# Turning attention probabilities from a rounded-kind view of the score tile, with explicit waits on their writers

## The chip, the cores and the metric

The kernel runs on one core of one Trainium2 chip. The metric is the device time of one execution in microseconds (us); the time before is the median of three runs. A core has a matrix engine (TensorE, PE in the profile, with its weight loads listed apart as PEld), a vector engine (VectorE, DVE), a scalar engine (ScalarE, ACT), a general engine (GpSimd, POOL) and a sequencer that only issues DMAs (SyncE, SP). Each works through its own queue in order; semaphores tie the queues together. SBUF is the memory that engines work in, PSUM the one that TensorE writes.

## The reference, cut to what matters

One layer of an encoder is applied to two groups of tokens, 1024 and 256, with shared weights: `x + W_out @ concat[SSD, windowed attention, memory attention]` of the normalized `x`. The two attentions are what the change touches:

```
# windowed grouped-query attention, 8 heads, 2 key/value heads, blocks of 128 queries
logits = where(|t-s| <= 128, q.k * d**-0.5 - slope*|t-s|, -inf)
m      = max(max(logits), sink)
probs  = exp(logits-m) / (sum(exp(logits-m)) + exp(sink-m))
o_att  = (probs @ v) * silu(z_att)
...
# memory cross-attention, 4 heads, 256 memory rows
pm     = softmax(mq.mk * d**-0.5)
o_mem  = (pm @ mv) * silu(z_mem)
```

Everything is float32. The kernel keeps that accuracy in the large products by splitting each operand into a rounded part (kind `fp32r`) and a rest, and adding three products of such parts.

## The kernel before

**Tiling and stages.** The 1280 tokens are ten tiles of 128 (`NT = 10`), in two groups of five. Most of the time goes into the projections: `block_tok`, `block_feat` and `block_pair` walk the 2048 input features in steps, load a tile of weights (`wraw`, a ring of four buffers), let ACT round it (`wh`, L206) and DVE take the rest (`wl`, L207), and issue three matmuls per product (L258 to L260, L293 to L295, L1268 to L1270) into PSUM tiles `acc`.

**What runs beside them.** Attention and the SSD scan are generators that wait in two queues (`lanes`) and are advanced a few steps at each step of a projection (`pump`, rates in `RATES`). The instructions that a step issues go to their engines' queues among those of the projection. The final order on each engine is set by a scheduler that works from priorities and its own cost estimates, so a change of an instruction's kind or of a dependency can also swap neighbours elsewhere.

**The windowed attention,** `attn(t)`, runs once per token tile, from 637 to 1304 us of the profile. After the queries are normalized (POOL computes `qr` at L123, L124 and L637, DVE applies it at L641) it makes four rounds `rr`. In `scores(rr)` POOL copies the sink into the last column of a score tile `lg` (L665), TensorE makes the scores `psc` (L671, L672), DVE adds the distances and writes `lg` (L673), ACT takes the exponential in place (L677) and DVE scales it in place by the reciprocal of the sum (L681). In `turn_(rr)` TensorE turns the probabilities, 128 columns at a time, into the PSUM tile `ppt` (L693), and ACT copies that to `pT` (L694). `values` multiplies by the values (L703). With two or three key blocks per tile there are 4 or 6 turns per round, 208 in all.

**The memory attention,** `mem_attn(t)`, does the same in two rounds `hp` per token tile: ACT writes the exponentials `mpr` (L781), DVE scales them (L786), and TensorE turns them into `pmt` (L794), 8 per tile and 80 in all.

A turn is a matmul whose weights are the piece of the probabilities and whose moving operand is the identity. The identity lies in a tile of kind `fp32r`, `identr`; `ident` is the same memory seen as float32. The turns of queries, keys, gates and SSD tiles (`pq` L653, `pk` L536, `pmq` L744, `pxs` L889, `pd` L1074, `pz` L1088) already use `identr` with an operand of kind `fp32r`; those of the probabilities and of the SSD result (`pr` L1038) use `ident` with a float32 operand.

Score tiles of both attentions come from one ring of two buffers with the tag `lg`, which a row of scales, `rbc`, also uses for a while. A tile's buffer is given to the next tile once every reader of the old one is done; the first instruction that writes into the buffer waits for that.

Of the kernel before, what the change touches and what calls it, by code (L numbers as in the profile page):

```python
# [10 lines left out]
F32 = mybir.dt.float32  # L11
F32R = mybir.dt.float32r
# [4 lines left out]
ALU = mybir.AluOpType  # L17
AX = mybir.AxisListType

P = 128  # L20
# [24 lines left out]
def hymba_encoder_kernel(  # L45
# [7 lines left out]
    V, A, G, T, S = nc.vector, nc.scalar, nc.gpsimd, nc.tensor, nc.sync  # L53
# [33 lines left out]
    identr = const([P, P], "identr", F32R)  # L87
    ident = identr.bitcast(F32)
# [87 lines left out]
    rbc = {}  # L176
# [440 lines left out]
        yield  # L617


    def attn(t):  # L620
        lo, hi = (0, NS) if t < NS else (NS, NT)
        k0, k1 = max(lo, t - 1), min(hi, t + 2)
        na = k1 - k0
        nk = na * P
        d0 = (k0 - (t - 1)) * P
        s0 = k0 if t < 4 else k0 - 3
        grp, ti = divmod(t, 5)
        tc_ = slice(ti * P, (ti + 1) * P)
        q = taken("attn", t)
        yield  # L630
        sq = w2("sq")
        A.activation(sq, q, AF.Square)
        ss = sm.tile([P, 8], F32, tag="s8", name="qss", bufs=4)
        V.reduce_sum(out=ss, in_=hv(sq), axis=AX.X)
        r = sm.tile([P, 8], F32, tag="s8", name="qr", bufs=4)
        rsqrt(r, ss, 1.0 / 64, 8)
        G.tensor_tensor(out=r, in0=r, in1=steep, op=ALU.mult)  # L637
        for _ in range(3):
            yield
        q3 = hv(q)  # L640
        V.tensor_mul(q3, q3, hb(r, 8, 64))  # L641
        yield
        qT = []
        for b in range(2):
            qh = mp.tile([P, 4, 2, 64], F32R, tag="wa", name="qh", bufs=WA)
            qb = q3[:, 4 * b:4 * b + 4, :]
            A.activation(qh[:, :, 0, :], qb, AF.Copy)
            V.tensor_sub(qh[:, :, 1, :], qb, qh[:, :, 0, :].bitcast(F32))
            yield
            ps = psum("pq")  # L650
            qf = qh.rearrange("p a b d -> p (a b d)")
            for a in range(4):
                T.transpose(ps[:, a * P:(a + 1) * P].bitcast(F32R), qf[:, a * P:(a + 1) * P], identr)  # L653
            o = mp.tile([P, 512], F32R, tag="qT", name="qT", bufs=2)
            A.activation(o, ps, AF.Copy)
            qT.append(o)
        z = w2("za")
        S.dma_start(hv(z, 4), zT_d[0][grp][:, :, tc_])
        yield
        ns8 = nsink.rearrange("p (v r) -> p r v", v=2)  # L660
        state_ = {}

        def scores(rr):
            lg = mp.tile([P, 2, 385], F32, tag="lg", name="lg", bufs=2)
            G.tensor_copy(lg[:, :, nk:nk + 1], ns8[:, rr, :].unsqueeze(2))  # L665
            nm = sm.tile([P, 2], F32, tag="m2", name="nm", bufs=10)
            for kv in range(2):
                h = 4 * kv + rr
                ps = psum("psc")
                st = qT[kv][:, rr * P:(rr + 1) * P]  # L670
                T.matmul(ps[:, :nk], st, kT[:, kv, s0 * P:s0 * P + nk], start=True, stop=False)  # L671
                T.matmul(ps[:, :nk], st, kL[:, kv, s0 * P:s0 * P + nk], start=False, stop=True)  # L672
                V.tensor_tensor_reduce(out=lg[:, kv, :nk], in0=pdist[:, d0:d0 + nk], in1=ps[:, :nk], scale=2.0 ** -(h + 1),  # L673
                                       scalar=nsink[:, h:h + 1], op0=ALU.add, op1=ALU.min, accum_out=nm[:, kv:kv + 1])
            den = sm.tile([P, 2], F32, tag="m2", name="den", bufs=10)
            for kv in range(2):
                A.activation(lg[:, kv, :nk + 1], lg[:, kv, :nk + 1], AF.Exp, scale=-1.0, bias=nm[:, kv:kv + 1],  # L677
                             accum_out=den[:, kv:kv + 1])
            V.reciprocal(out=den, in_=den)
            for kv in range(2):  # L680
                V.tensor_scalar(out=lg[:, kv, :nk], in0=lg[:, kv, :nk], scalar1=den[:, kv:kv + 1], scalar2=0.5,  # L681
                                op0=ALU.mult, op1=ALU.mult)
            state_[rr] = lg

        def turn_(rr):
            lg = state_.pop(rr)
            if rr % 2 == 0:
                state_["pT"] = mp.tile([P, 2, 2, 384], F32, tag="pT", name="pT", bufs=1)
            pT = state_["pT"]
            for kv in range(2):  # L690
                pt = psum("ppt")
                for a in range(na):
                    T.transpose(pt[:, a * P:(a + 1) * P], lg[:, kv, a * P:(a + 1) * P], ident)  # L693
                A.activation(pT[:, kv, rr % 2, :nk], pt[:, :nk], AF.Copy)  # L694

        oT = w2("oT")

        def values(half):
            pT = state_.pop("pT")
            po = psum("po")  # L700
            for a in range(na):
                for kv in range(2):
                    T.matmul(hv(po[kv * 64:kv * 64 + 64, :2 * P], 2), v_all[:, s0 + a, kv * 64:kv * 64 + 64],  # L703
                             pT[:, kv, :, a * P:(a + 1) * P], start=(a == 0), stop=(a == na - 1))
            c = slice(half * 2 * P, (half + 1) * 2 * P)
            V.tensor_mul(oT[:, c], po[:, :2 * P], z[:, c])

        scores(0)
        yield
        scores(1)  # L710
        yield
        yield
        turn_(0)
        yield
        scores(2)
        yield
        turn_(1)
        yield
        scores(3)
        yield  # L720
        values(0)
        yield
        turn_(2)
        yield
        turn_(3)
        yield
        fetch_next()
        yield
        values(1)
        yield  # L730
        S.dma_start(oT_d[0][grp][:, :, tc_], hv(oT, 4))


    def mem_attn(t):
# [29 lines left out]
        st_ = {}  # L764

        def scores(hp):
            ps = psum("pms")
            for j in range(2):
                h = 2 * hp + j
                c = slice(h * P, (h + 1) * P)  # L770
                o = ps[:, j * 256:(j + 1) * 256]
                T.matmul(o, qh[:, c], mkH[:, h, :], start=True, stop=False)
                T.matmul(o, qh[:, c], mkL[:, h, :], start=False, stop=False)
                T.matmul(o, ql[:, c], mkH[:, h, :], start=False, stop=True)
            m = sm.tile([P, 2], F32, tag="m2", name="mm", bufs=10)
            V.reduce_max(out=m, in_=hv(ps, 2), axis=AX.X)
            V.scalar_tensor_tensor(out=m, in0=m, scalar=-1.0, in1=r[:, 2 * hp:2 * hp + 2], op0=ALU.mult, op1=ALU.mult)
            pr = mp.tile([P, 512], F32, tag="lg", name="mpr", bufs=2)
            den = sm.tile([P, 2], F32, tag="m2", name="mden", bufs=10)
            for j in range(2):  # L780
                A.activation(pr[:, j * 256:(j + 1) * 256], ps[:, j * 256:(j + 1) * 256], AF.Exp,  # L781
                             scale=r[:, 2 * hp + j:2 * hp + j + 1], bias=m[:, j:j + 1], accum_out=den[:, j:j + 1])
            V.reciprocal(out=den, in_=den)
            for j in range(2):
                c = slice(j * 256, (j + 1) * 256)
                V.tensor_scalar(out=pr[:, c], in0=pr[:, c], scalar1=den[:, j:j + 1], scalar2=0.5,  # L786
                                op0=ALU.mult, op1=ALU.mult)
            st_[hp] = pr

        def turn_(hp):  # L790
            pr = st_[hp]
            pt = psum("pmt")
            for a in range(4):
                T.transpose(pt[:, a * P:(a + 1) * P], pr[:, a * P:(a + 1) * P], ident)  # L794
            if hp == 0:
                st_["pT"] = mp.tile([P, 2, 768], F32, tag="pT", name="mpT", bufs=1)
            pT = st_["pT"][:, hp, :512]
            A.activation(pT, pt, AF.Copy)
            st_[hp] = pT
# [659 lines left out]
    def x_rows(grp):  # L1459

        yield
        yield
        rbc[grp] = fin.tile([P, 640], F32, tag="rbc", name="rbc") if grp == 0 else \
            mp.tile([P, 640], F32, tag="lg", name="rbc", bufs=2)
        for o, n in ((0, 4), (4, 1)):
            ps = psum("prx")
            for i in range(n):
                t = 5 * grp + o + i
                T.matmul(ps[:, i * P:(i + 1) * P], rx[:, t:t + 1].broadcast_to([P, P]), ident, start=True, stop=True)
            V.tensor_copy(rbc[grp][:, o * P:(o + n) * P], ps[:, :n * P])  # L1470
        yield
# [289 lines left out]
```

## Time and profile before

| | |
|---|---|
| runs before, median of 3 (lowest, highest) | 1787.72 us (1787.32, 1790.27) |
| profiled execution, first to last instruction | 1784.2 us |
| median of the runs less that span | 3.5 us |
| TensorE busy | 1774.6 us, 99% of the span, 10838 matmuls |
| VectorE / ScalarE / GpSimd busy | 70% / 52% / 31% |
| granted TensorE clock, mean | 1.000 |

The profile holds one execution. Its times are counted from the first instruction; no time of that execution outside the span is recorded, so its own time is its span and whatever lies around it, for which the 3.5 us to the median of the runs is the only measure. A group row reads: line, engine, operation, what is written <- what is read, shape, count | busy time, mean duration in ns of one | idle time of the engine just before. Matmuls overlap in the array, so the duration of one is longer than the step from one to the next.

### The profile page before, as it was taken

What the parts mean: (1) busy time and instruction counts of PE and PEld (TensorE: products, weight loads), DVE (VectorE), ACT (ScalarE), POOL (GpSimd) and SP (SyncE); (2) the same over time, 40 slices, a digit from 0 to 9 for tenths busy, and PEclk for the clock granted to TensorE, in tenths of its full rate; (3) what the DMA queues carried; (4) which work ended last, traced back from release to release, by engine and by line L of the source; (5) the groups of instructions that cost most, each with busy time, mean ns of one, the idle gap of its engine ahead of it and who ended that gap; (6) DMA issues with size and microseconds to landing.
All of it is one profiled execution on the core that took longest, in us unless ns stands there. A gap on an engine that the chain in (4) does not pass through costs nothing.

```text
span 1784.2 us, 31407 instructions
## 1 busy us (share of the span) xinstructions
PE 1774.6 (99%) x10838; PEld 1606.3 (90%) x10838; DVE 1245.8 (70%) x2358; ACT 921.5 (52%) x2049; POOL 547.3 (31%) x900
## 2 busy tenths in 40 slices
PE   9999999999999999999999999999999999999999
PEld 7889999999998999999889977877988888899999
DVE  5596788888768887777665666557777644766665
ACT  5555455555434766756464565544447533533333
POOL 0105789999810100001001010000100000057775
PEclk9999999999999999999999999999999999999999
DMA  8654454445446644453635645557777764744442
GB/s 299 191 183 125 135 154 148 141 146 159 126 144 205 199 134 139 135 162 110 189 118 175 193 148 160 168 158 249 229 229 242 247 189 140 224 147 142 148 142 78
DMA packets 208207, 301.12 MB, mean 169 GB/s; under 512 B 19568, under 2 KB 86192, under 8 KB 208048
## 3 DMA queue, kind: packets, MB, share of 16 engines
q1 hardware_dynamic: 207904, 299.06, 54.5%
q8 instruction: 85, 1.39, 0.3%
q14 instruction: 74, 0.61, 0.1%
q10 hardware_dynamic: 144, 0.06, 0.0%
HBM read 236.36 MB, written 62.69 MB: 168 GB/s over the span
## 4 chain that ended last, share of the span: by engine, by line
PE 82%; issue 6%; DVE 4%; DMA 4%; POOL 2%; ACT 1%; SPq 0%; POOLq 0%; ACTq 0%; DVEq 0%
PE acc L258 9%; PE acc L260 8%; PE acc L259 8%; PE acc L1268 7%; PE acc L1270 7%; PE acc L1269 7%; PE acc L293 5%; PE acc L295 5%; PE acc L294 5%; PE accm L1268 3%; PE accm L1269 3%; PE accm L1270 3%; PE po L703 1%; PE ppt L693 1%; PE py L970 1%
## 5 line engine op out<-in xcount | busy, mean ns | idle before, releaser
L207 DVE TENSOR_TENSOR wl<-wraw,wh 128x512 fp32r<-128x512 f32 (+1 forms) x480 | 346.2, 723 | 244.0 <-ACT wh L206 238.5
L206 ACT ACTIVATE wh<-wraw 128x512 fp32r<-128x512 f32 (+1 forms) x480 | 292.2, 613 | 312.4 <-PE acc L260 147.8
L258 PE MATMUL acc<-wh,xH 128*128 128x512 f32 (+1 forms) x1088 | 418.9, 385 | 0.4 <-DVE v_all L337 0.4
L260 PE MATMUL acc<-wh,xL 128*128 128x512 f32 (+1 forms) x1088 | 410.1, 377 | 0.0
L259 PE MATMUL acc<-wl,xH 128*128 128x512 f32 (+1 forms) x1088 | 409.7, 377 | 0.0
L258 PEld LDWEIGHTS acc<-wh,xH 128*128 128x128 f32 x1088 | 204.5, 188 | 37.8 <-issue 3.4
L260 PEld LDWEIGHTS acc<-wh,xL 128*128 128x128 f32 x1088 | 204.4, 188 | 37.0 <-issue 0.2
L259 PEld LDWEIGHTS acc<-wl,xH 128*128 128x128 f32 x1088 | 204.7, 188 | 35.9 <-issue 1.6
L293 PE MATMUL acc<-xH,wh 128*128 128x320 f32 x640 | 202.8, 317 | 0.0
L294 PE MATMUL acc<-xL,wh 128*128 128x320 f32 x640 | 198.8, 311 | 0.0
L295 PE MATMUL acc<-xH,wl 128*128 128x320 f32 x640 | 198.0, 309 | 0.0
L206 ACT ACTIVATE sh<-ws 128x384 fp32r<-128x384 f32 x176 | 91.3, 523 | 204.8 <-POOL ws L1236 102.5
L207 DVE TENSOR_TENSOR sl<-ws,sh 128x384 fp32r<-128x384 f32 x176 | 123.8, 706 | 94.6 <-ACT sh L206 94.4
L1236 POOL TENSOR_TENSOR ws<-wraw 128x128 f32<-128x128 f32 x176 | 110.8, 630 | 205.8 <-DMA wraw<-in_w_in_pairs_dram 80.9
L665 POOL COPY lg<-nsink 128x2 f32<-128x2 f32 x40 | 13.6, 340 | 379.1 <-PE ppt L693 221.3
L1236 POOL TENSOR_TENSOR ws<-wraw,ws 128x128 f32<-128x128 f32 x176 | 118.7, 674 | 13.8
L293 PEld LDWEIGHTS acc<-xH,wh 128*128 128x128 f32 x640 | 120.2, 188 | 2.8 <-issue 2.2
L294 PEld LDWEIGHTS acc<-xL,wh 128*128 128x128 f32 x640 | 120.3, 188 | 1.7 <-issue 1.4
L295 PEld LDWEIGHTS acc<-xH,wl 128*128 128x128 f32 x640 | 120.2, 188 | 0.6 <-issue 0.5
L1236 POOL TENSOR_TENSOR wraw<-wraw 128x128 f32<-128x128 f32 x176 | 112.9, 642 | 13.7
L1236 POOL TENSOR_TENSOR ws<-ws,wraw 128x128 f32<-128x128 f32 x176 | 115.6, 657 | 0.0
L362 DVE SCALAR_TENSOR_TENSOR c<-u,vec,c 128x638 f32<-128x638 f32 (+1 forms) x96 | 90.0, 938 | 9.9 <-ACT c L357 9.5
(437 smaller groups left out, 3942.7 us busy)
## 6 DMA issues: line engine op xcount, KB each, us to landing
wraw<-in_w_in_laid_dram SPq DMA_DIRECT2D x176, 256.0 KB, 3.0
wraw<-in_w_in_pairs_dram SPq DMA_DIRECT2D x112, 256.0 KB, 2.7
wraw<-in_w_out_laid_dram SPq DMA_DIRECT2D x64, 256.0 KB, 3.5
wraw<-in_w_out_pairs_dram SPq DMA_DIRECT2D x64, 256.0 KB, 2.8
rf<-ac SPq DMA_DIRECT2D x40, 256.0 KB, 4.1
rb<-ac SPq DMA_DIRECT2D x40, 256.0 KB, 4.7
wraw<-in_w_mem_laid_dram SPq DMA_DIRECT2D x32, 256.0 KB, 4.4
xst<-in_x_sample_dram SPq DMA_DIRECT2D x20, 256.0 KB, 5.9
```

The lines of the kernel that those rows point to most:

```text
L206: a = A.activation(h, raw, AF.Copy)
L207: b = V.tensor_sub(l, raw, h.bitcast(F32))
L258: T.matmul(ps[t][:, :n], sh, h[:, :n], start=(k_ == 0), stop=False)
L259: T.matmul(ps[t][:, :n], sh, l[:, :n], start=False, stop=False)
L260: T.matmul(ps[t][:, :n], sl, h[:, :n], start=False, stop=(k_ == KT - 1))
L293: T.matmul(o, sh, cur["H", q][:, m, c], start=(k == 0), stop=False)
L294: T.matmul(o, sh, cur["L", q][:, m, c], start=False, stop=False)
L295: T.matmul(o, sl, cur["H", q][:, m, c], start=False, stop=(k == KT - 1))
L1236: G.tensor_tensor(out=o, in0=x, in1=y, op=op)
L1268: T.matmul(ps[p], h, xh, start=(k_ == 0), stop=False)
L1269: T.matmul(ps[p], h, xl, start=False, stop=False)
L1270: T.matmul(ps[p], l, xh, start=False, stop=(k_ == 7))
```

## The change

The probability tiles get a second name. After `scores` has written a tile, `turn_` asks the pool for a new tile of kind `fp32r` under the same tag, that is in the same memory, and turns from that with `identr` in place of `ident`. The tool that orders the instructions tracks tiles, not memory, so three things are added:

- each of the two buffers gets a tag of its own, `lg0` and `lg1`, with one buffer each, and the tiles take them in turn (`score_tile`); `rbc` of the second token group takes `lg0`;
- the new tile gets a writer of its own, a POOL memset of its last column (`as_words`), which lies outside what the turns read; it waits for all users of the old tile;
- each turn is told by hand to wait for the DVE instruction that scaled the piece it reads (`turn_words`).

The computed function is the same: turning does not change the words.

```diff
+    def score_tile(name, shape):
+        place[0] ^= 1
+        tag = f"lg{place[0]}"
+        return tag, mp.tile([P] + shape, F32, tag=tag, name=name, bufs=1)
+
+    def turn_words(out, words, wrote):
+        i = T.transpose(out.bitcast(F32R), words, identr)
+        for w in wrote:
+            tc.add_manual_dep(i.ins, w.ins.name, WRITTEN, reason="the words' writer")
+
+    def as_words(tag, name, shape):
+        w = mp.tile([P] + shape, F32R, tag=tag, name=name, bufs=1)
+        G.memset(w.bitcast(F32)[(slice(None),) + tuple(slice(n - 1, n) for n in shape)], 0.0)
+        return w
...
         def scores(rr):
-            lg = mp.tile([P, 2, 385], F32, tag="lg", name="lg", bufs=2)
+            tag, lg = score_tile("lg", [2, 385])
...
         def turn_(rr):
-            lg = state_.pop(rr)
+            tag, wrote = state_.pop(rr)
+            lg = as_words(tag, "lgw", [2, 385])
...
-                    T.transpose(pt[:, a * P:(a + 1) * P], lg[:, kv, a * P:(a + 1) * P], ident)
+                    turn_words(pt[:, a * P:(a + 1) * P], lg[:, kv, a * P:(a + 1) * P], wrote[kv:kv + 1])
...
-            pr = mp.tile([P, 512], F32, tag="lg", name="mpr", bufs=2)
+            tag, pr = score_tile("mpr", [512])
...
+            pr = as_words(tag, "mprw", [513])
...
-                T.transpose(pt[:, a * P:(a + 1) * P], pr[:, a * P:(a + 1) * P], ident)
+                turn_words(pt[:, a * P:(a + 1) * P], pr[:, a * P:(a + 1) * P], wrote[a // 2:a // 2 + 1])
...
-            mp.tile([P, 640], F32, tag="lg", name="rbc", bufs=2)
+            mp.tile([P, 640], F32, tag="lg0", name="rbc", bufs=1)
```

In the changed file the turns have line 632, the memset 639, the sink copy 687, the score matmuls 693 and 694, and the last step of `qr` 659.

**The turns on TensorE.** One round of the second token tile, `attn(1)`, with what each instruction waits for in brackets. Before:

```order
L295 MATMUL acc<-xH_7440,wl 128x320
L693 MATMUL ppt<-identr,lg 128x128 [waits DVE_49,Activation_49]
L693 MATMUL ppt<-identr,lg 128x128 x2
L693 MATMUL ppt<-identr,lg 128x128 [waits DVE_49]
L671 MATMUL psc<-kT,qT 128x384 [waits DVE_49]
L672 MATMUL psc<-kL,qT 128x384
```

The same place in the changed program:

```order
L295 MATMUL acc<-xH_7440,wl 128x320
L632 MATMUL ppt<-identr,lgw 128x128 [waits DVE_49,Activation_49]
L632 MATMUL ppt<-identr,lgw 128x128 x2
L632 MATMUL ppt<-identr,lgw 128x128 [waits DVE_49]
L693 MATMUL psc<-kT,qT 128x384 [waits DVE_49]
L694 MATMUL psc<-kL,qT 128x384
```

The place in the queue and the engines waited for are the same; no turn waits for POOL, since the memset writes a column that no turn reads.

**The memsets and sink copies on POOL.** The stretch from the queries' normalization of `attn(1)` to that of `attn(2)` (`qr` is the scale that DVE applies to the queries, `lg` a score tile, `lgw` its second name). Before:

```order
L637 TENSOR_TENSOR qr<-qr,steep 128x8
L665 COPY lg<-nsink 128x2 x4
L123 TENSOR_SCALAR qr<-qss 128x8
L124 TENSOR_TENSOR qr<-qr,mhalf 128x8
L637 TENSOR_TENSOR qr<-qr,steep 128x8
```

With the change:

```order
L659 TENSOR_TENSOR qr<-qr,steep 128x8
L687 COPY lg<-nsink 128x2
L639 MEMSET lgw 128x1 x2
L687 COPY lg<-nsink 128x2
L639 MEMSET lgw 128x1
L687 COPY lg<-nsink 128x2 x2
L639 MEMSET lgw 128x1
L687 COPY lg<-nsink 128x2
L123 TENSOR_SCALAR qr<-qss 128x8
L124 TENSOR_TENSOR qr<-qr,mhalf 128x8
L659 TENSOR_TENSOR qr<-qr,steep 128x8
```

Four memsets stand between the copies, and a fifth copy, that of the second round of `attn(2)`, has moved from behind that tile's `qr` chain to ahead of it. Elsewhere on POOL there is a memset for each of the 60 score tiles, and the neighbours keep their order but for three other exchanges of a copy with one instruction. On TensorE 34 matmuls stand some rows earlier or later; on DVE, ACT and SP some dozens of rows are exchanged with neighbours.

More of the change, by code (lines that the diff above doesn't have):

```diff
@@ L617, in dt_prep @@
         yield
+    place = [0]
+    def score_tile(name, shape):
+        place[0] ^= 1
+        tag = f"lg{place[0]}"
+        return tag, mp.tile([P] + shape, F32, tag=tag, name=name, bufs=1)
+    WRITTEN = mybir.DependencyInfo(mybir.DependencyClass.Sync, mybir.DependencyReason.DATA)
+    def turn_words(out, words, wrote):
[6 more added lines that the diff above has]
+        return w
     def attn(t):
@@ L679, in scores @@
             V.reciprocal(out=den, in_=den)
[L680 to L683, printed above, removed]
+            wrote = [V.tensor_scalar(out=lg[:, kv, :nk], in0=lg[:, kv, :nk], scalar1=den[:, kv:kv + 1], scalar2=0.5,
+                                     op0=ALU.mult, op1=ALU.mult) for kv in range(2)]
+            state_[rr] = tag, wrote
         def turn_(rr):
-            lg = state_.pop(rr)
+            tag, wrote = state_.pop(rr)
+            lg = as_words(tag, "lgw", [2, 385])
             if rr % 2 == 0:
@@ L783, in scores @@
             V.reciprocal(out=den, in_=den)
+            wrote = []
             for j in range(2):
                 c = slice(j * 256, (j + 1) * 256)
-                V.tensor_scalar(out=pr[:, c], in0=pr[:, c], scalar1=den[:, j:j + 1], scalar2=0.5,
-                                op0=ALU.mult, op1=ALU.mult)
-            st_[hp] = pr
+                wrote.append(V.tensor_scalar(out=pr[:, c], in0=pr[:, c], scalar1=den[:, j:j + 1], scalar2=0.5,
+                                             op0=ALU.mult, op1=ALU.mult))
+            st_[hp] = tag, wrote
         def turn_(hp):
-            pr = st_[hp]
+            tag, wrote = st_[hp]
+            pr = as_words(tag, "mprw", [513])
             pt = psum("pmt")
             for a in range(4):
-                T.transpose(pt[:, a * P:(a + 1) * P], pr[:, a * P:(a + 1) * P], ident)
+                turn_words(pt[:, a * P:(a + 1) * P], pr[:, a * P:(a + 1) * P], wrote[a // 2:a // 2 + 1])
             if hp == 0:
```

## Prediction

> **What bounds the kernel now.** I read the page first: busy times, the clock by slices, the chain that ended last.
>
> ```profile
> PE 1774.6 (99%) x10838; PEld 1606.3 (90%) x10838; DVE 1245.8 (70%) x2358; ACT 921.5 (52%) x2049; POOL 547.3 (31%) x900
> PEclk9999999999999999999999999999999999999999
> PE 82%; issue 6%; DVE 4%; DMA 4%; POOL 2%; ACT 1%; SPq 0%; POOLq 0%; ACTq 0%; DVEq 0%
> ```
>
> TensorE holds 82% of the chain, and its clock is full. Since its busy time is modelled, 99% alone proves little. The list of waits of TensorE is better evidence; it is short, and these are its longest entries:
>
> ```profile
> PE pmt L794 <- DVE mpr L786: 1.4, 2, 1.3
> PE warm L1544 <- DVE zero L1542: 1.3, 1, 1.3
> PE acc L1268 <- ACT qs L326: 0.8, 1, 0.8
> ```
>
> Idle time is 1784.2 - 1774.6 = 9.6 us in all, no DMA is among the releasers, and a turn of the probabilities waited 1.4 us in total. The stretch with all attention, one row of the table of windows (busy time of PE, PEld, DVE, ACT, POOL, then clock), says the same where the change lies:
>
> ```profile
> 637.00:1467.00 830.00, 826.88 (x5074) 717.38 (x5073) 561.62 (x1228) 467.77 (x1159) 66.39 (x120) 1.00 0.57 177
> ```
>
> TensorE idles 3.1 of 830 us; DVE has 268 us free, ACT 362, POOL 764. So what is taken off TensorE here should come off the end, and what is put on the others has room, unless a queue's order makes someone wait.
>
> **The turns.** The groups by shape give the counts, with two kinds of turn that already read `fp32r`:
>
> ```profile
> L693 PE MATMUL ppt<-identr,lg 128*128 128x128 f32 x208 | 31.2, 277 | 0.0
> L794 PE MATMUL pmt<-identr,mpr 128*128 128x128 f32 x80 | 11.4, 273 | 1.4 <-DVE mpr L786 1.4
> L1074 PE MATMUL pd<-identr,ydT 128*128 128x128 f32 x80 | 10.1, 249 | 0.5 <-DVE nm L673 0.5
> L653 PE MATMUL pq<-identr,qh 128*128 128x128 f32 x80 | 9.0, 246 | 0.0
> ```
>
> 288 turns change kind; 277 against 246 ns would be 31 ns each, or 8.9 us, but those are durations of overlapping matmuls. What counts is the time from the start of a group of turns until the matmuls behind it are back in step. I take it from the timeline, in four places where the projection L258 to L260 lies on both sides: from the start of the turns to the start of the second matmul after them. First float32 groups of 8 and 4, then `fp32r` groups of 8 and 4:
>
> ```profile
> 1438.94 1.03 PE L794 MATMUL pmt<-identr,mpr 128*128 128x128 f32 x8
> 1439.73 0.48 PE L258 MATMUL acc<-wh,xH 128*128 128x512 f32 x1
> 1440.05 0.39 PE L259 MATMUL acc<-wl,xH 128*128 128x512 f32 x1
> ...
> 1496.47 0.60 PE L1038 MATMUL pr<-identr,yd 128*128 128x128 f32 x4
> 1497.14 0.39 PE L259 MATMUL acc<-wl,xH 128*128 128x512 f32 x1
> ...
> 1065.84 0.79 PE L653 MATMUL pq<-identr,qh 128*128 128x128 f32 x8
> 1066.77 0.39 PE L259 MATMUL acc<-wl,xH 128*128 128x512 f32 x1
> ...
> 1486.56 0.46 PE L1074 MATMUL pd<-identr,ydT 128*128 128x128 f32 x4
> 1487.16 0.39 PE L259 MATMUL acc<-wl,xH 128*128 128x512 f32 x1
> ```
>
> Eight turns: 1440.05 - 1438.94 = 1.11 us against 1066.77 - 1065.84 = 0.93, so 0.18 less. Four: 0.67 against 0.60, so 0.07 less. An added float32 turn costs (1.11 - 0.67)/4 = 0.110 us, an added `fp32r` turn (0.93 - 0.60)/4 = 0.083. On the line through both, n turns in a row gain 0.0275 n - 0.04 us: 0.015 for 2, 0.04 for 3, 0.125 for 6. In the changed order of TensorE the windowed attention's turns stand in 22 groups of 6, 10 of 4, 6 of 3 and 9 of 2, the memory attention's in 5 of 8, 9 of 4 and 2 of 2; the sum is 22 x 0.125 + 19 x 0.07 + 6 x 0.04 + 11 x 0.015 + 5 x 0.18 = 2.75 + 1.33 + 0.24 + 0.17 + 0.90 = 5.4 us. All of it lies on the engine that bounds. The rate of 4 for all 288 turns gives 5.0 us, that of 8 gives 6.5; both round to the trace's hundredths.
>
> [...]
>
> **The waits on the turns.** A turn waited for DVE before and waits for DVE now, and takes no wait on POOL: nothing added on this path. The extra wait in the bound is that of each buffer's next writer, on the memset.
>
> **Sixty memsets on POOL,** not seen in this trace for this place. The nearest row is the sink copy, of similar size:
>
> ```profile
> L665 POOL COPY lg<-nsink x40: 181/188/942, 511.5 to 1288.4; 128x2 f32<-128x2 f32 x40
> ```
>
> At 0.19 us each they are 11.3 us of POOL's 764 free. Three parties can be held up. The next user of the buffer is DVE two score tiles later; the tightest case is here, between the scaling of one tile (L681) and the first write into the same buffer (the last row):
>
> ```profile
> 740.63 0.74 DVE L681 TENSOR_SCALAR lg<-lg,den 128x384 f32<-128x384 f32 x2
> 745.76 0.62 DVE L673 CUSTOM_DVE_ANT_0 lg<-pdist,psc,nsink 128x384 f32<-128x384 bf16 x1
> ```
>
> The memset can start at 741.4 and is due at 745.8: 4.4 us for 0.2. Next, the exponential needs the sink copy, which a memset may now precede; the tightest case:
>
> ```profile
> 785.49 0.51 POOL L665 COPY lg<-nsink 128x2 f32<-128x2 f32 x1 [24.98 <-PE ppt L693]
> 786.58 0.62 ACT L677 ACTIVATE lg<-lg,nm 128x385 f32<-128x385 f32 x1 [0.60 <-DVE nm L673]
> ```
>
> It is 0.58 us early, and before it POOL had been waiting 25 us, long enough for any memset. So I take zero for all sixty; the ends are zero and 11.3 us, the price if TensorE waited out each.
>
> [...]
>
> **The moved copy.** In `attn(2)` the second round's sink copy now precedes that tile's `qr` chain. It waits for the last turns of `attn(1)`, and behind it stand `qr`, then L641 on DVE, then whatever DVE does next:
>
> ```profile
> 702.74 0.82 PE L693 MATMUL ppt<-identr,lg 128*128 128x128 f32 x6
> ...
> 702.42 0.20 POOL L123 TENSOR_SCALAR qr<-qss 128x8 f32<-128x8 f32 x1 [2.03 <-DVE qss L634]
> 704.41 0.54 POOL L637 TENSOR_TENSOR qr<-qr,steep 128x8 f32<-128x8 f32 x1
> ...
> 704.99 0.69 DVE L641 TENSOR_TENSOR q<-q,qr 128x512 f32<-128x512 f32 x1
> 705.60 0.89 DVE L362 SCALAR_TENSOR_TENSOR c<-u,vec,c 128x646 f32<-128x646 f32 x1
> 707.64 0.69 DVE L207 TENSOR_TENSOR wl<-wraw,wh 128x512 fp32r<-128x512 f32 x1 [1.16 <-ACT wh L206]
> ```
>
> The turns end at 703.6, the copy at about 703.8, so L123 starts 1.4 us later than 702.42, and L641 and L362 with it. DVE then has 1.16 us of idle before the next weight split L207, which would come some 0.2 us late, with at least one split tile still ahead of TensorE. I take zero; the ends are zero and 1.4 us.
>
> **Other moves.** Neighbours are exchanged on SP, DVE, ACT and TensorE. TensorE waited for no DMA before, and each exchange is of one instruction (0.2 to 0.9 us in the rows above) whose sum of idle is 9.6 us over the whole run; I take 0 with ends of -2 and +3 us. Buffers that strictly alternate replace a ring of two: the tiles come and go in turn, so I take zero.
>
> **Sum:** 5.4 us off the span of 1784.2, which gives 1778.8; with the 3.5 us between span and median, 1787.7 - 5.4 = 1782.3 us.
>
> **Rivals.**
> - *Gain given back.* TensorE runs ahead, and the weight splits then end last. For it: DVE waits for ACT's rounding at L207 in the last row, so the splits are only just in time in places. Against it: TensorE's waits are 9.6 us in all. At half the gain: 1785.0 us, no measurable change.
> - *The turns do not get faster,* because the new view runs at the old rate. Against it: L653 and L1074 have the same form. Time 1787.7.
> - *POOL becomes a link in the path* (the other side). If copies that wait for turns stand ahead of `qr` in all ten tiles, and DVE stops at L641 each time for the chain's 2.5 us (702.42 to 704.95), TensorE runs out of split weights: 25 us, so 1787.7 - 5.4 + 25 = 1807 us. It decides from about 0.9 us per tile on. Against it: one such copy has clearly moved, and an idle gap behind it covers it.
>
> **How the numbers follow.** A difference of 0.2%, 3.6 us, is about what a measurement of this kernel can tell from none. The forecast has 0.72; gain given back 0.18; no faster turns 0.04; POOL in the path 0.06. The forecast itself spreads by the ends above, 5.0 to 6.5 us of gain and -2 to +3 of the exchanges, so it lies between 1779 and 1786, and some of it falls within 0.2%. Faster 0.68, the same 0.25, slower 0.07. The range is 1779.5 to 1787.2: down to the gain of 6.5 with most of the favourable exchanges, up to where nearly nothing is left.
>
> **What would show it.** Right: the turns (now L632) 288 times at about 246 ns instead of 275; a group of 8 to the second matmul after it in 0.93 us; sixty memsets near 0.2 us with no DVE or ACT wait on them; the window of attention some 5 us shorter with TensorE's idle still near 3 us. Wrong: L641 or L673 waiting for POOL, new TensorE waits for DVE splits, or turns that still take 275 ns.

## The result, and the profile after

| | before | change | ratio, 95% interval |
|---|---|---|---|
| first comparison, median | 1787.64 us | 1782.84 us | 0.9976 (0.9966 to 0.9986) |
| second | 1786.73 us | 1781.84 us | 0.9973 (0.9962 to 0.9983) |
| third | 1787.34 us | 1782.44 us | 0.9976 (0.9966 to 0.9986) |

The change is faster by 4.8 to 4.9 us. The forecast was 1782.3 us. The profiled execution of the change took 1784.35 us with a span of 1782.6, so 1.7 us lie around the span. The busy times of its page:

```profile
PE 1770.5 (99%) x10838; PEld 1602.9 (90%) x10838; DVE 1243.3 (70%) x2358; ACT 920.3 (52%) x2049; POOL 550.2 (31%) x960
```

The groups by shape, the turns of both attentions:

```profile
L632 PE MATMUL ppt<-identr,lgw 128*128 128x128 f32 x208 | 25.4, 249 | 0.0
L632 PE MATMUL pmt<-identr,mprw 128*128 128x128 f32 x80 | 9.2, 246 | 1.3 <-DVE mpr L809 1.3
```

The view of one tile (shortest, median and longest in ns, first and last start), and the top of TensorE's list of waits:

```profile
L639 POOL MEMSET lgw<- x40: 95/98/101, 634.2 to 1292.0; 128x1 f32 x40
```
```profile
PE pst L920 <- ACT fh L934: 2.0, 1, 2.0
```

285 of the 288 turns last 0.22 to 0.29 us. Three last about 0.62 us; each of them is the first turn behind `pyf` (L937), a matmul of 0.59 us. POOL has sixty instructions more, of 98 ns each, and the view of L639 lists no instruction that waited for one. TensorE's longest wait is new: 2.0 us for ACT's `fh`, a tile of the SSD scan. That one wait distorts this profile. The windows around it (columns as in the prediction: length, PE, PEld, DVE, ACT, POOL, granted clock, DMA share, GB/s):

```profile
1341.00:1344.10 3.10, 1.09 (x12) 0.82 (x10) 3.10 (x5) 2.99 (x8) 0.00 (x0) 1.00 1.02 350
1344.10:1346.10 2.00, 2.00 (x8) 1.60 (x9) 1.61 (x4) 2.00 (x6) 0.00 (x0) 0.86 1.06 385
1346.10:1348.10 2.00, 2.00 (x6) 1.62 (x5) 1.71 (x3) 2.00 (x6) 0.00 (x0) 0.50 1.06 367
1348.10:1350.10 2.00, 2.00 (x9) 1.56 (x9) 1.57 (x3) 0.42 (x2) 0.00 (x0) 0.79 0.83 294
```

After the wait the granted clock stands at half for 0.56 + 2.00 + 0.84 = 3.4 us (a mean of 0.86 in 2 us is 0.56 us at half, 0.79 is 0.84 us). The steps of L258 to L260 are 0.43 us there and 0.23 us outside, so at a work rate of about half the stretch costs some 1.7 us, and with the wait 3.7. So a second profile of the same kernel is the better one to read, of an execution with no such stretch. The turns of the windowed attention by tile, in the profile of before, in the first of the change, and in the second:

```profile
L693 PE MATMUL ppt<-identr,lg x208: 270/273/331, 637.5 to 1303.8; 128*128 128x128 f32 x104
```
```profile
L632 PE MATMUL ppt<-identr,lgw x208: 220/248/625, 637.4 to 1299.9; 128*128 128x128 f32 x104
```
```profile
L632 PE MATMUL ppt<-identr,lgw x208: 221/248/626, 637.1 to 1298.8; 128*128 128x128 f32 x104
```

The second profile's busy times, window of attention and wait for `fh`:

```profile
span 1778.0 us, 31504 instructions
PE 1768.6 (99%) x10838; PEld 1601.3 (90%) x10838; DVE 1245.9 (70%) x2358; ACT 920.8 (52%) x2049; POOL 549.4 (31%) x960
```
```profile
637.00:1467.00 830.00, 826.52 (x5107) 717.42 (x5106) 563.43 (x1232) 468.93 (x1161) 72.71 (x179) 1.00 0.57 179
```
```profile
PE pst L920 <- ACT fh L934: 0.6, 1, 0.6
```

From the first to the last windowed turn it was 666.3 us before, and is 662.5 and 661.7 us. In the first profile the 3.9 us gained by then (1303.8 - 1299.9) are met by the some 3.7 us lost at 1344, and with what the last turns bring 1.6 us are left at the end (1784.2 - 1782.6). In the second the span is 6.2 us shorter. TensorE idles 830 - 826.52 = 3.5 us in the window of attention, against 3.1 before. Over the whole span its busy time fell from 1774.6 to 1768.6 us, and its idle time is 9.4 us after 9.6: the time left TensorE's work, not its waits.

### The profile page after: what moved, and what is told of

Its sections match the earlier page's. It is cut to its first block, busy times and chain, and to the rows that moved or that the text cites. A ratio compares the mean times of both kernels' runs of the same rounds, so it can differ in the third digit from the quotient of the medians.

```text
span 1782.6 us, 31504 instructions
## 1 busy us (share of the span) xinstructions
PE 1770.5 (99%) x10838; PEld 1602.9 (90%) x10838; DVE 1243.3 (70%) x2358; ACT 920.3 (52%) x2049; POOL 550.2 (31%) x960
## 4 chain that ended last, share of the span: by engine, by line
PE 85%; issue 6%; DVE 3%; DMA 3%; ACT 2%; POOL 1%; SPq 0%; ACTq 0%; POOLq 0%; DVEq 0%
PE acc L258 10%; PE acc L260 10%; PE acc L259 10%; PE acc L1294 7%; PE acc L1292 7%; PE acc L1293 7%; PE acc L293 5%; PE acc L294 4%; PE acc L295 4%; PE accm L1293 3%; PE accm L1292 3%; PE accm L1294 3%; PE po L725 1%; PE py L994 1%; PE pmo L833 1%
## 5 line engine op out<-in xcount | busy, mean ns | idle before, releaser
L207 DVE TENSOR_TENSOR wl<-wraw,wh 128x512 fp32r<-128x512 f32 (+1 forms) x480 | 347.2, 725 | 243.9 <-ACT wh L206 238.7
L258 PE MATMUL acc<-wh,xH 128*128 128x512 f32 (+1 forms) x1088 | 419.2, 385 | 0.3 <-DVE v_all L337 0.3
L260 PE MATMUL acc<-wh,xL 128*128 128x512 f32 (+1 forms) x1088 | 410.6, 378 | 0.0
L258 PEld LDWEIGHTS acc<-wh,xH 128*128 128x128 f32 x1088 | 204.8, 188 | 37.9 <-issue 3.3
L260 PEld LDWEIGHTS acc<-wh,xL 128*128 128x128 f32 x1088 | 204.7, 188 | 37.3 <-issue 0.6
L293 PE MATMUL acc<-xH,wh 128*128 128x320 f32 x640 | 203.1, 317 | 0.0
L295 PE MATMUL acc<-xH,wl 128*128 128x320 f32 x640 | 198.0, 309 | 0.0
L207 DVE TENSOR_TENSOR sl<-ws,sh 128x384 fp32r<-128x384 f32 x176 | 121.4, 693 | 96.5 <-ACT sh L206 93.8
L293 PEld LDWEIGHTS acc<-xH,wh 128*128 128x128 f32 x640 | 120.2, 188 | 3.0 <-issue 2.5
L295 PEld LDWEIGHTS acc<-xH,wl 128*128 128x128 f32 x640 | 120.2, 188 | 0.3 <-issue 0.2
L639 POOL MEMSET lgw<- 128x1 f32 x40 | 3.9, 98 | 291.0 <-DVE lg L702 224.5
```

The lines of the kernel that those rows point to most:

```text
L207: b = V.tensor_sub(l, raw, h.bitcast(F32))
L258: T.matmul(ps[t][:, :n], sh, h[:, :n], start=(k_ == 0), stop=False)
L260: T.matmul(ps[t][:, :n], sl, h[:, :n], start=False, stop=(k_ == KT - 1))
L293: T.matmul(o, sh, cur["H", q][:, m, c], start=(k == 0), stop=False)
L295: T.matmul(o, sl, cur["H", q][:, m, c], start=False, stop=(k == KT - 1))
```

## The experiments

**The turns back to float32, with all else of the change kept.**

```
-        i = T.transpose(out.bitcast(F32R), words, identr)
+        i = T.transpose(out, words.bitcast(F32), ident)
```

> The change with all its parts (own slots for each score tile, a second tile in the slot, memsets, explicit waits), but the turns read that tile as float32, as before. Theory A (the gain is the kind of the turn, summed over the groups of turns on TensorE): 1787.6 us, the time of the kernel before; the turns' rows go back to 275 ns. Theory B (the gain is the new order that the slots and waits bring on the engines, and the kind adds little): 1782.8 us, the time of the change. The memsets alone, if they cost TensorE anything, would show here as more than 1787.6.

Measured: 1786.98 us against 1786.73 before, ratio 1.0004 (0.9995 to 1.0013). The turns' group is back at the old duration; behind it, a row of TensorE's waits:

```profile
L632 PE MATMUL ppt<-identr,lgw 128*128 128x128 f32 x208 | 31.4, 277 | 0.0
```
```profile
PE pst L920 <- ACT fh L934: 1.4, 1, 1.4
```

Theory B falls. Slots, memsets, explicit waits and the new order together are worth between -0.9 and +2.3 us, and the kind of the turn makes the gain. The second row is a small cost of the new order: the wait for `fh` is in this profile too, and in the list of waits of the one profile of before it is missing.

**Each turn issued twice,** in the change (the turn and its waits in a loop of two) and in the kernel before:

```
+                    for _ in range(2):
                         T.transpose(pt[:, a * P:(a + 1) * P], lg[:, kv, a * P:(a + 1) * P], ident)
```

> The change with each of its 288 fp32r turns issued twice in a row into the same place (work doubled, result the same). Theory A: an added fp32r turn costs 0.083 us on the engine that bounds, 288 x 0.083 = 23.9, so 1782.8 + 23.9 = 1806.7 us. Theory B (turns lie in gaps of TensorE, or the splits of weights end last): clearly less than 23.9 us more. If the groups' rows understate a turn, the time of its own row, 248 ns, is the upper end: 71 us more.

> The kernel before with each of its 288 float32 turns issued twice in a row into the same place (work doubled, result the same). Theory A: an added float32 turn costs 0.110 us, 288 x 0.110 = 31.7, so 1787.6 + 31.7 = 1819.3 us; against the doubled fp32r turns the distance grows from 4.8 to 12.6 us. Theory B (the kind adds little): the doubled turns cost the same in both kernels, and the distance stays 4.8 us. [...]

Measured: 1806.19 us, which is 24.4 over the change (1781.84), 0.085 us for an added `fp32r` turn; and 1817.43 us, 30.7 over before (1786.73), 0.107 us for an added float32 turn. Theory A gave 0.083 and 0.110. The distance between the kernels grew from 4.9 to 11.2 us. TensorE's idle time is 11.2 and 10.2 us in the two profiles, against 9.4 in the change's second and 9.6 before, so nearly all that was added is busy time. An added turn lies on the path that sets the end, in both kernels, and its price is the step between turns, a little over a third of its row's duration of 249 or 274 ns. With four executions each the prices are not sharp: the interval of the ratio puts the float32 one between 0.099 and 0.118 us. The bound from the row's duration (71 us) falls.

**The change once more,** for a second profile.

> The changed kernel once more, for a second profile and more times. In the first profile TensorE lost about 3 of the gained 3.9 us near 1344 us: it waited 2.0 us for ACT's fh tile, and then ran a few us at a granted clock of about 0.6. Theory A: that is an accident of the profiled execution (transfers that came late); the second profile doesn't have it, and its span is 1779 to 1781 us. Theory C: the new order sets it up, so it is there again, and the turns' gain is in truth larger than the time shows.

Measured: 1781.84 us, span 1778.0, which is 1 us below theory A's 1779 to 1781. But the wait for `fh` did not vanish: 0.6 us here, 2.0 in the first profile, 1.9 in a third, 1.4 with float32 turns. So it seems to belong to the new order, with a size that varies from execution to execution; what is accidental is the stretch at half clock behind it, which neither the second nor the third profile has (the last section sets the third's wait beside the first's). Neither theory was right as it stood.

**More memsets.** Each memset nine times, then sixty times:

```
+        for _ in range(9):
             G.memset(w.bitcast(F32)[(slice(None),) + tuple(slice(n - 1, n) for n in shape)], 0.0)
```

> The change with each of its sixty memsets issued nine times in a row: 480 more memsets of 98 ns, 47 us of work on POOL, 0.88 us in a row at each score tile. Theory A (the memsets lie in POOL's idle time, tightest slack 4.4 us before DVE's next write into the slot): 1782 us, no change against the changed kernel, at most 1 us more. Theory D (POOL is a link in the path: sink copies and the chain behind the score tiles come late by the memsets in front of them): up to 60 x 0.78 = 47 us more, and at least 5 us.

> The change with each memset issued sixty times: 5.9 us in a row on POOL at each score tile, 347 us in all, more than the tightest slack of 4.4 us and less than POOL's idle time. Theory A: the slack is per tile and the tightest tiles now make DVE, ACT and then TensorE wait, so it is slower: 5 to 40 us over the changed kernel's 1782; the most would be 60 x 5.8 = 347 us. Theory E (only POOL's total matters): no change.

Measured: nine times, 1781.84 us, the same as the change, at a ratio of 0.9972 (0.9963 to 0.9982) to before. The groups show 36.8 + 18.6 = 55.4 us of memsets, against 60 x 98 ns = 5.9 in the change:

```profile
L640 POOL MEMSET lgw<- 128x1 f32 x360 | 36.8, 103 | 289.7 <-DVE lg L703 183.8 <-ACT lg L700 30.3 <-ACT rb L984 29.7
L640 POOL MEMSET mprw<- 128x1 f32 x180 | 18.6, 104 | 121.1 <-DVE mpr L810 101.2 <-DVE mm L800 8.5 <-PE pmt L632 1.9
```

Theory D falls for bursts of 0.9 us: DVE waits 0.9 us in all for the memsets at L696, and the end does not move. Sixty times: 1834.29 us, 52.5 over the change and more than the 5 to 40 expected. POOL is busy 864.0 of 1832.7 us, so theory E (the total) falls: it is the order and the time of each burst that matter. Who waited, of DVE, ACT and TensorE:

```profile
DVE lg L696 <- POOL lgw L640: 34.5, 15, 5.8
DVE yd L1054 <- POOL yrs L1134: 27.4, 9, 10.8
DVE q L664 <- POOL lgw L640: 14.7, 5, 5.8
ACT lg L700 <- POOL lgw L640: 45.0, 14, 4.9
PE psc L694 <- DVE nm L696: 6.1, 2, 5.2
```

Three of these rows are the parties that the prediction named: the next writer of the slot (L696), the `qr` chain (here L664 on DVE), and the exponential behind the sink copy (L700). The second row is one that it did not name: `yrs`, a scale of the SSD result, which POOL computes and DVE applies at L1054; that wait was 17.2 us in the change's second profile. One stretch of the timelines of POOL, DVE and TensorE shows such a chain, for TensorE's longest wait. Two bursts stand one behind the other on POOL (the view begins inside the first of them). Behind them come the last steps of `yrs`, with a sink copy (L688) among them. DVE waits 5.86 us at L1054 for `yrs`, its next instruction is the score tile (L696), and TensorE waits for that:

```profile
1254.83 7.23 POOL L640 MEMSET lgw<- 128x1 f32 x62
...
1262.67 5.24 POOL L640 MEMSET lgw<- 128x1 f32 x34
...
1268.95 0.19 POOL L688 COPY lg<-nsink 128x2 f32<-128x2 f32 x1
1269.10 0.22 POOL L1134 TENSOR_SCALAR yrs<-yrs 128x2 f32<-128x2 f32 x1
```
```profile
1269.35 0.49 DVE L1054 TENSOR_SCALAR yd<-yd,yrs 128x512 f32<-128x512 f32 x1 [5.86 <-POOL yrs L1134]
1269.75 0.47 DVE L696 CUSTOM_DVE_ANT_0 lg<-pdist,psc,nsink 128x256 f32<-128x256 bf16 x1
```
```profile
1270.29 0.58 PE L694 MATMUL psc<-kT,qT 128*128 128x256 f32 x1 [5.24 <-DVE nm L696]
```

So here POOL's order, and not the memory slot, carried the delay. Other waits came straight from the slot: up to 1158.59 us TensorE stood still for 3.3 us, behind a score tile (L696) that DVE could write only after a burst.

The expectation left out the clock. The page's busy times, and the window right behind this wait, with the clock at half:

```profile
PE 1787.3 (98%) x10838; PEld 1613.4 (88%) x10838; DVE 1246.1 (68%) x2358; ACT 920.3 (50%) x2049; POOL 864.0 (47%) x4500
```
```profile
1270.29:1272.29 2.00, 2.00 (x6) 1.71 (x7) 1.93 (x7) 1.86 (x5) 0.60 (x7) 0.50 0.03 8
```

TensorE's idle time is 1832.7 - 1787.3 = 45.4 us against 1778.0 - 1768.6 = 9.4 in the change's second profile, 36.0 more, and its busy time for the same matmuls is 18.7 us more; together they are the 54.7 us between the two spans. Its mean clock is 0.991; if what is missing was spent at half, that is 0.009 x 1832.7 / 0.5 = 33 us, and by an estimate at half the work rate it cost 16.5, most of the 18.7. So the waits alone stay inside 5 to 40, and the clock adds about half as much again.

**The turns' kind by another way:** the scaling writes into a rounded tile of its own, and score tiles have one slot instead of two.

```
-            lg = mp.tile([P, 2, 385], F32, tag="lg", name="lg", bufs=2)
+            lg = mp.tile([P, 2, 385], F32, tag="lg", name="lg", bufs=1)
...
+            lw = mp.tile([P, 2, 384], F32R, tag="lw", name="lw", bufs=1)
             for kv in range(2):
-                V.tensor_scalar(out=lg[:, kv, :nk], in0=lg[:, kv, :nk], ...
+                V.tensor_scalar(out=lw[:, kv, :nk], in0=lg[:, kv, :nk], ...
...
-                    T.transpose(pt[...], lg[:, kv, a * P:(a + 1) * P], ident)
+                    T.transpose(pt[...].bitcast(F32R), lw[:, kv, a * P:(a + 1) * P], identr)
```

> Another way to the same turns: the kernel before, in which the scaling of the probabilities writes into a tile of its own of the rounded kind (one slot), and the turns read that; one slot instead of two for the score tile. The probabilities are rounded to the fp32r kind by the scaling, which the change doesn't do. No memset, no explicit wait, no second tile in the slot. Theory A (the gain is the turns' kind): 1782 us, as with the change, give or take 1.5 for the single slots. Theory F (a score tile must now wait until the scaling of the tile ahead has ended, and a scaling until the turns of the tile ahead): TensorE gets new waits, and the time is 1785 us or more.

Measured: 1784.63 us against 1786.52 us before in the same comparison, ratio 0.9989 (0.9980 to 0.9997), about 2.8 us behind the change, though the interval of the change's ratio (0.9962 to 0.9983) just overlaps with this one. The turns are as fast (248 ns), but TensorE has new waits, led by the memory attention's turns, and 14.6 us of idle time in all:

```profile
PE pmt L796 <- DVE mpw L788: 2.1, 3, 1.4
PE pmt L796 <- ACT rb L961: 1.4, 1, 1.4
PE pd L1076 <- DMA ydT<-yd: 1.3, 1, 1.3
```

Theory F is nearer. This profile is of the slowest execution of its eleven (1788.43 us), so the rows tell where it waits and not how much in the median; that the single slots cause all 2.8 us is not shown.

**The change carried on to the SSD result,** `pr`, the last large group of float32 turns:

```
...
+            y = as_words(("ya" if t % 2 else "rf") + str(g), "ydw", [513])
             ps = psum("pr")
             for j in range(4):
-                T.transpose(ps[:, j * P:(j + 1) * P], y[:, j * P:(j + 1) * P], ident)
+                turn_words(ps[:, j * P:(j + 1) * P], y[:, j * P:(j + 1) * P], [w])
```

> The change carried on to the turns of the state part's result (80 turns in 20 groups of 4, float32 in both kernels): they too read a rounded-kind tile that lies in the slot of the normalized result, with 20 more memsets and explicit waits, and the slots written out as pairs. Theory A: 20 groups at 0.07 us each, 1.4 us less than the changed kernel, so 1780.4 us; by the doubled turns' prices (0.022 us a turn) 80 x 0.022 = 1.8 us less. Theory G: these turns stand where TensorE waits for others (its longest wait in two of the runs is behind this place), so nothing changes against 1781.8 us.

> The changed kernel a third time, only to have more times beside those of the run below. Theory A: 1781.8 us median, as the last time.

> The version that also turns the state part's result from a rounded-kind tile, again, since its first times (1781.4 against 1781.8 us) did not tell it from the change. Theory A: 1.4 us less than the change, 1780.4 us. Theory G (these turns stand where TensorE has to wait anyway): no difference from the change, 1781.8 us.

Measured: 1781.40 against 1781.84 us, then 1782.60 against 1782.44. Over all times of these four runs the median is 1782.0 us for both kernels (21 and 15 executions). The groups did get quicker, as in this pair of timelines, the change first (the start of four turns, and the second matmul behind them):

```profile
1490.46 0.60 PE L1062 MATMUL pr<-identr,yd 128*128 128x128 f32 x4
...
1491.13 0.39 PE L259 MATMUL acc<-wl,xH 128*128 128x512 f32 x1
```
```profile
1490.54 0.46 PE L632 MATMUL pr<-identr,ydw 128*128 128x128 f32 x4
...
1491.14 0.39 PE L259 MATMUL acc<-wl,xH 128*128 128x512 f32 x1
```

From the start to the second matmul it is 0.67 us, then 0.60, the price that the prediction took for four. But TensorE now waits for the copy `so` of just these turns:

```profile
PE pyb L1116 <- ACT so L1065: 1.3, 1, 1.3
```

It is 0.8 us in this kernel's second profile; in the change it was 0.5 us in the first profile and is missing from the second's and third's lists, and before it was 0.6. That speaks for theory G, turns that end sooner and then wait for ACT; but it is less than 1.4 us, and with times that spread over 8 us a gain of a few tenths stays open. No version was measured to be clearly faster than the change.

## Why the prediction was right, point by point

- **The bound.** TensorE sets the end: added turns cost their full step in both kernels (0.085 and 0.107 us each), and what was taken off came off the end (in the second profile 6.0 us of TensorE's busy time and 6.2 of the span).
- **The price of a turn.** At a place of the same kind as the prediction's eight float32 turns, and at one with six turns between the shorter matmuls L293 to L295 (before, then the change's second profile):

```profile
743.80 0.82 PE L693 MATMUL ppt<-identr,lg 128*128 128x128 f32 x6
...
744.60 0.31 PE L294 MATMUL acc<-xL,wh 128*128 128x320 f32 x1
```
```profile
742.21 0.63 PE L632 MATMUL ppt<-identr,lgw 128*128 128x128 f32 x6
...
742.90 0.30 PE L294 MATMUL acc<-xL,wh 128*128 128x320 f32 x1
...
1433.31 0.80 PE L632 MATMUL pmt<-identr,mprw 128*128 128x128 f32 x8
...
1434.24 0.40 PE L259 MATMUL acc<-wl,xH 128*128 128x512 f32 x1
```

  Eight turns take 1434.24 - 1433.31 = 0.93 us, as forecast. Six gain 0.80 - 0.69 = 0.11 us, where 0.125 was forecast. Over all 22 groups of six in the profile of before and in the change's second, the median of this step is 0.85 and then 0.76 us, a gain of 0.09; for the groups of three and two it is next to nothing, where the line gave 0.04 and 0.015. Summed with the medians of all sizes that is about 4.3 us, so the term of 5.4 us was sized high, mostly at the groups of six. The doubled turns give 288 x 0.022 = 6.3 us instead, but they lengthen the groups, and their interval is wide. The time moved by 4.8 to 4.9. Its interval, 2.5 to 6.1 us in the first comparison, holds 4.3 and 5.4, so the turns' own share is not known to better than about a microsecond, nor what the wait for `fh` takes of it. That the forecast came within 0.6 us of the measured median is in part luck.
- **The factor between the kinds.** By the doubled turns a float32 turn costs 0.107 / 0.085 = 1.26 times an `fp32r` one; the prediction's prices, 0.110 and 0.083 us, give 1.33.
- **The memsets.** Price wrong by half, 98 ns instead of 190, taken from a copy; placed rightly at zero, which holds up to nine times the work. The slack of 4.4 us was that of the tightest tile in the old order (4.2 in the change's second profile); with 5.9 us in a row the waits reach 5.8 us, since bursts of two tiles can follow each other on POOL. DVE's own work did not lengthen beside the memsets: it is busy 1245.8 us before and 1246.1 with each memset issued sixty times.
- **The moved copy.** It now stands ahead of the `qr` chain. In the second profile, on POOL and on DVE:

```profile
702.21 0.19 POOL L687 COPY lg<-nsink 128x2 f32<-128x2 f32 x1 [1.84 <-PE ppt L632]
702.48 0.53 POOL L123 TENSOR_SCALAR qr<-qss 128x8 f32<-128x8 f32 x1
```
```profile
705.50 0.69 DVE L663 TENSOR_TENSOR q<-q,qr 128x512 f32<-128x512 f32 x1 [1.81 <-POOL qr L659]
706.11 0.89 DVE L362 SCALAR_TENSOR_TENSOR c<-u,vec,c 128x646 f32<-128x646 f32 x1
706.92 0.68 DVE L207 TENSOR_TENSOR wl<-wraw,wh 128x512 fp32r<-128x512 f32 x1
```

  L123 starts 0.06 us later than before instead of 1.4, because the turns that the copy waits for start at 701.45 us and not at 702.74. L663 waits 1.81 us, and the split L207 behind it comes at 706.92, ahead of the 707.64 of before, so nothing was lost here. In all, L663 waits 6.5 us for `qr`, where L641 waited 3.8 before: one of the prediction's signs of being wrong did grow, at a cost that the time does not show.
- **Exchanges of neighbours** were taken as zero with ends of -2 and +3 us. The float32 version puts them at -0.9 to +2.3, and the wait for `fh` is the one that was found.
- **Span and run.** The 3.5 us between the span and the median were taken as lying around the span. The execution's own time and span differ by 1.7 us in all later runs, so the profile of before was of an execution some 1.8 us below its median. As the gain was subtracted from the median, this did no harm.
- **Rivals.** "Gain given back" happened in part and at a place that was not named, L920 waiting for `fh`. "POOL a link in the path" exists as a mechanism, and where it begins to cost was not found: 0.88 us of memsets per score tile moved nothing, 5.9 us cost 52.5 us. The prediction's 0.9 us was another quantity, time that TensorE loses per token tile; none was lost.

## What to carry to other kernels

Price a short matmul by the step that it adds to its group, from its start to the second matmul behind it, and not by its row's duration: the step (0.085 and 0.107 us) told the time, the durations (249 and 274 ns) did not. Here, with TensorE busy to 99%, the cheaper kind of operand for the turns was worth the sixty memsets of 98 ns and the waits that it needs, which lay on an engine with 4.2 us of slack at the tightest tile; slack in total was not enough, since each memset issued sixty times cost 52.5 us with POOL busy 864.0 of 1832.7. And the last group of the same edit may give nothing: with the SSD result's turns it was 1782.0 us with and without, with a wait for `so` behind them of 1.3 and 0.8 us.

## What the hardware showed unexpectedly

In several profiles a short idle of TensorE cost twice: once as a wait, and again in 3.4 us at half the granted clock behind it. In the first profile of the change the stretch followed 2.0 us of idle; in the doubled `fp32r` turns 3.0 us (the wait, and the windows behind it):

```profile
PE pyb L1116 <- ACT so L1065: 3.0, 1, 3.0
```
```profile
1258.13:1260.13 2.00, 2.00 (x6) 1.49 (x7) 0.76 (x2) 0.56 (x2) 0.00 (x0) 0.73 0.44 129
1260.13:1262.13 2.00, 2.00 (x9) 2.00 (x9) 2.00 (x4) 0.00 (x0) 0.00 (x0) 0.50 0.86 177
1262.13:1264.13 2.00, 2.00 (x14) 1.68 (x14) 0.33 (x1) 0.51 (x1) 0.00 (x0) 0.91 0.78 293
```

Here 1.08 + 2.00 + 0.36 = 3.4 us again. The length of the wait alone did not decide. In the third profile of the change TensorE waited 1.95 us for `fh`, up to 1343.17 us, and the clock stayed full:

```profile
1338.52:1341.93 3.41, 2.70 (x18) 2.15 (x16) 2.96 (x6) 2.59 (x7) 0.00 (x0) 1.00 0.99 315
1341.93:1345.34 3.41, 2.17 (x9) 1.72 (x10) 2.31 (x4) 3.41 (x10) 0.00 (x0) 1.00 1.08 381
1345.34:1348.76 3.42, 3.42 (x23) 3.04 (x22) 3.42 (x6) 3.41 (x10) 0.00 (x0) 1.00 0.87 301
```

The bounds of these rows are not chosen freely. In the clock records of all twelve traces every change of the granted clock comes a whole number of 3.413 us steps after the first change (392, 393 and 520 in the first profile of the change, 521 in that of before); in the run with sixty memsets the half stretches begin 188, 200, 208, 236, 307, 361, 370 and 390 steps after it, and each lasts one step or two. So in these traces the changes lie on a grid that runs on through work and waits alike. In the third profile a line of that grid, carried on to 1341.93, cuts the wait into 0.71 us of idle time in one step and 1.24 in the next. In the first profile nearly all of the 2.0 us lie in the one step from 1342.13 to 1345.54, and the clock is at half in the next. In the version with a rounded tile of its own, a step with 1.67 us of idle time (851.08 to 854.50) is followed by half clock and one with 1.40 (1346.02 to 1349.43) is not. There is no sharp limit in these numbers: in the run with sixty memsets a step with 1.46 us was followed by half clock, and two neighbouring ones with 1.65 and 1.67, a wait of 3.3 us cut by a line at 1156.92, were not. Why one step was followed by half clock and another was not, these traces do not show.
